# Three order edits around the last carry and the last merge of a hybrid RWKV-7 / neighbourhood-attention layer: one PSUM evacuation placed earlier, VectorE's order in the last gate written out by hand, one weight's low half made by an adding DMA

## The chip, the cores and the metric

The kernel runs on one core of a Trainium2 chip. The metric is the device time of one execution in microseconds, taken as the median of the runs shown. The engines have these names: PE is TensorE (matmul; PEld is its weight load), DVE is VectorE, ACT is ScalarE, POOL is GpSimd, SP is SyncE, which here does nothing but issue DMAs. Each engine works through its own queue in order.

## The reference, cut to what matters

One layer acts on 512 latent tokens and 128 context tokens, which the kernel treats as one block of 640 columns. The part that matters here is how the layer's two branches are merged:

```python
h = _rmsnorm(x, p["norm1_g"]) * (1.0 + sc1) + sh1
u_rw, u_na, gate_rw, gate_na = jnp.split(h @ p["w_in"], IN_SPLITS, axis=-1)
o_rw, s_new = _rwkv_branch(u_rw, s0, ...)
...
merged = (jax.nn.sigmoid(gate_rw) * (o_rw @ p["w_o_rwkv"])
          + jax.nn.sigmoid(gate_na) * (o_na @ p["w_o_na"]))
x = x + g1 * (merged @ p["w_out"])
h2 = _rmsnorm(x, p["norm2_g"]) * (1.0 + sc2) + sh2
x = x + g2 * ((jax.nn.silu(h2 @ p["ffn_w1"]) * (h2 @ p["ffn_w3"])) @ p["ffn_w2"])
```

The state recurrence inside `_rwkv_branch` runs forwards and backwards over the tokens, with a 64x64 state for each of 8 heads.

## The kernel before

All data is fp32. A product with a weight is made of three matmuls on operands split into a rounded high part and a low part (the rest): high times high, high times low and low times high. The weight's split is `wcast` (line 178). ACT writes the high half (`whi`, line 185). The low half (`wlo`) is made in one of two ways: by a DVE subtraction (line 188), or, where `eng is pool`, by ACT writing minus the weight's high part (line 183) and a DMA issued from POOL's queue that adds the weight itself (line 184). The weights come from HBM into `wst` buffers by DMAs on SP's queue (line 167), and a buffer is loaded anew once its readers are done.

The recurrence is done in chunks of 64 tokens for four pairs of heads, `ct` 0 to 3. For each pair there is a `carry` (line 1342): eight hops that pass the state from chunk to chunk. A hop is a short chain over engines: PE (L1367) into PSUM, ACT copies `x` (L1370), PE again (L1394), ACT copies `ZV` (L1400), PE (L1407, L1424), DVE multiplies the decay into the next `ZV` (L1419), and the next hop's PE work starts.

The hops leave PE idle, so the function `weave` (line 1560) puts other matmuls between their steps. They come from one long stream, `fill`, which makes projections, gates and the merges with `w_o`. The merge tasks are `merge_gen` (line 1509): matmuls into one of two PSUM buffers named `fl`, then an evacuation `rest` that frees the buffer, as `act.copy` into `mt` for the attention part (line 1524; the tiles of `mt` reuse others' memory and so carry names such as `kk` or `bv` in the profile) and as two DVE operations for the recurrence part (lines 1528 and 1530). An evacuation is not issued where its matmuls end. `later` puts it into the list `pend` with a delay counted in fill matmuls, and during a carry (`hold`) it is issued by `beside` at the places that the table `PRM["plan"]` sets: each step of the table is a number of fill matmuls, a dot, and a number that chooses a budget for ACT and DVE work (0 for none).

Behind the last carry (`ct` 3) comes its output stage (`out`, L1440 to L1455), then the last piece of the merge, here called the last gate, `last_gen` (line 1642). Sixteen times (8 tiles of 128 channels, two halves of 320 tokens), PE makes three matmuls into one of three PSUM buffers (L1652), DVE multiplies with the gate (L1653, which reads PSUM and so frees the buffer), DVE adds the sum so far (L1655, both inputs in SBUF), ACT rounds to the high part (L1656), and POOL subtracts to get the low part (L1657). The gates come back from HBM as `pre` and `tr` (L1646). From the sixth half on, two matmuls of the product with `w_out` (`acc`, L303, made by `tok_gen`) follow each half's three. The product is done in two passes of four weight pieces: `w_out[0]` to `w_out[3]` make output columns 0 to 511, `w_out[4]` to `w_out[7]` the rest. The first pass makes low halves by adding DMAs, the second by DVE.

What sets the order: inside a `manual_schedule` the named engines run in the order of the Python text, and every other engine's instructions are ordered by the tile framework's scheduler. For the last gate only PE is named (`MANUAL`).

Of the kernel before, what the change touches and what calls it, by code (L numbers as in the profile page):

```python
# [49 lines left out]
        ("0.0.0 16.1.0 8.1.1 9.0.0 2.1.0 8.1.1 13.1.1 0.1.1 0.1.1 0.1.1 0.1.0 6.1.0 6.1.0 6.1.0 6.1.0 "  # L50
         "6.1.0 6.1.0 7.1.0 6.0.0 6.0.0 6.0.0 6.0.0 6.0.0 6.0.0 7.0.0 6.0.0 6.0.0 6.0.0 6.0.0 6.0.0 "
         "6.0.0 6.0.0 11.0.0 8.0.0 8.0.0 2.0.0 0.0.0"),
        ("10.0 0.0 6.1 4.2 0.0 6.1 4.2 0.0 6.1 4.2 0.0 6.1 4.2 0.0 6.1 4.2 0.0 6.1 4.2 0.0 6.1 4.2 0.0 "
         "6.1 8.2 6.0"),
        "2 0 6 6 6 4 4 5 2 0 5 1 1 0 0"),
    qp=((0, 0, 7, 6, 7), (2, 5, 4, 4, 3, 2, 5, 3, 1)), ada=2, pa=1, pd=0,
# [21 lines left out]
MANUAL = {mybir.EngineType.PE}  # L78
# [29 lines left out]
def body(ctx: ExitStack, tc: tile.TileContext, xs, xp, cols, consts, w_ada, b_row, w_rw, w_qkv,  # L108
# [3 lines left out]
    pe, act, dve, pool, sp = nc.tensor, nc.scalar, nc.vector, nc.gpsimd, nc.sync  # L112
# [44 lines left out]
    def wdma(src, home=None):  # L157
        if len(rot) > 1 and home is None:
            rot.append(rot.pop(0))
        pl, nst, nhl = (rot if home is None else wpool)[-1 if home is None else home] if rot else wpool[-1]  # L160
        st = pl.tile([P, 1024], F32, tag="wst", bufs=nst, name=nm("wst"))
        n = src.shape[1]
        if len(src.shape) == 3:
            sp.dma_start(V(st[:, :], [[src.shape[2], n], [1, src.shape[2]]]), src)
            n *= src.shape[2]
        else:
            sp.dma_start(st[:, :n], src)
        return st, n, pl, nhl

    pend, off, hold, gtag = [], [0], [False], ["fl"]  # L170
# [7 lines left out]
    def wcast(w, eng=None):  # L178
        st, n, pl, nhl = w
        hi = pl.tile([P, 1024], F32R, tag="whi", bufs=nhl, name=nm("whi"))  # L180
        lo = pl.tile([P, 1024], F32R, tag="wlo", bufs=nhl, name=nm("wlo"))
        if eng is pool:
            act.activation(lo[:, :n], st[:, :n], AF.Copy, scale=-1.0)  # L183
            pool.dma_start(lo[:, :n].bitcast(F32), st[:, :n], accum_op=ALU.add)
        act.copy(hi[:, :n], st[:, :n])  # L185
        if eng is not pool:
            def low(a, b):
                dve.tensor_tensor(out=lo[:, a:b], in0=st[:, a:b], in1=hi[:, a:b].bitcast(F32), op=ALU.subtract)  # L188

            if len(gtag) > 1:  # L190
                low(0, 512)
                later(lambda: low(512, n), (0, 0), -off[0] + 5)
            else:
                low(0, n)
        return hi, lo

    def wload(src, eng=None):
        return wcast(wdma(src), eng)
# [22 lines left out]
    def drain(g):  # L221
        for _ in g:
            pass
# [50 lines left out]
    def tok_block(*args, **kw):  # L274
        pss = {}
        for _ in tok_gen(pss, *args, **kw):
            pass
        return pss
# [151 lines left out]
    def blkch(b):  # L430
        return [w_qkv[b * 4 + q] for q in range(4)]
# [74 lines left out]
    def tick(n):  # L506
        for p in pend:
            p[0] -= n
        while pend and pend[0][0] <= (-24 if hold[0] else 0):
            pend.pop(0)[2]()  # L510

    def beside(gen, budget):

        a = d = 0
        while a < budget[0] and d < budget[1]:
            if pend and pend[0][0] <= 0:
                _, c, fn = pend.pop(0)
                fn()
            else:
                c = next(gen, None)  # L520
                if c is None:
                    return
            a, d = a + c[0], d + c[1]
# [299 lines left out]
    with s1:  # L823
# [25 lines left out]
        with s1a:  # L849
            for b, dst, gcol in ((0, qT, dcol(dqg)), (1, kT, col("kg"))):  # L850
                pss = tok_block(pp, (hh, hl), blkch(b), list(range(8)), range(5)) if b else psq
# [44 lines left out]
            pss = tok_block(pp, (hh, hl), blkch(2), list(range(8)), range(5))  # L896
# [20 lines left out]
        with ExitStack() as s1b:  # L917
# [127 lines left out]
            with tc.manual_schedule(engines=FIRST):  # L1045
                for k, step in enumerate(PRM["na"].split()):
                    a, p, b, q, n = (int(x) for x in step.split("."))
# [29 lines left out]
    with ExitStack() as s3:  # L1077
# [482 lines left out]
        def weave(gen, others=(), bud=None):  # L1560

            for _ in (_ for g in ((0,), gen, (0,)) for _ in g):
                p = next(plan)
                for _ in range(p[0]):
                    if not next(fill, False):
                        break
                for o_, n in zip(others, p[1:]):
                    if bud:
                        if n:
                            beside(o_, bud[n - 1])  # L1570
                        continue
                    for _ in range(n):
                        next(o_, None)
                tick(PRM["tk"])
# [86 lines left out]
    def w_out_gen(pss, ws, toks, **kw):  # L1661
        return tok_gen(pss, pp, (mh, ml), ws, list(range(8)), toks, **kw)

    pss = {}
    trp = open_pool(hs, "trp")
    weights(hs, 2, 2)
    w0 = w_out_gen(pss, [c0] + [w_out[q] for q in range(1, 4)], range(5), eng=pool)
    with tc.manual_schedule(engines=MANUAL):
        for h, _ in enumerate(last_gen()):
            for _ in range(PRM["lw"][h]):  # L1670
                next(w0)
        drain(w0)
# [121 lines left out]

    with tc.manual_schedule(engines=FIRST):
        w1s = []
        beside(w_out_gen(pss, [w_out[4 + q] for q in range(4)], (0, 1, 2), tail=2, keep=w1s))
        beside(w_out_gen(pss, w1s, (3, 4), tail=2))
    hstack.close()

# [149 lines left out]
    with tc.manual_schedule(engines=FIRST):  # L1950
# [6 lines left out]
        for part, fs in enumerate(fts):  # L1957
# [13 lines left out]
            for n in range(2):  # L1971
                fin = part == len(fts) - 1 and n == 1
                pss = {}
# [121 lines left out]
```

## Time and profile before

| what | value |
|---|---|
| median of 3 runs | 1171.36 us (1169.81 to 1171.37) |
| the profiled execution, its own time | 1167.39 us |
| its span from first to last instruction | 1165.6 us |
| PE, PEld, DVE, ACT, POOL busy | 1119.1, 992.5, 778.7, 532.4, 191.2 us |
| mean granted TensorE clock | 0.995 |
| last carry (first hop's PE work to the last ACT copy of its output) | about 606.9 to 640.4 us |
| last gate (first to last of its matmuls) | 657.7 to 673.8 us |
| first matmul with `w_out` | 662.2 us |

The table's last three rows are read from the timeline. A row of the timeline gives the start and the length of one instruction or of a run of equal ones (x3), the engine, the line, the output and input tiles, and in brackets how long the engine had been idle before it and whose work ended that. The lengths of neighbouring matmuls overlap, so the distance between starts tells their pace. A row of the windows view gives a stretch, its length, and each engine's busy time with its count of instructions, then the granted PE clock, the busy share of the DMA engines and the bytes that they moved.

### The profile page before, as it was taken

The numbers are of one execution on the slowest core, as the hardware profiler recorded it, in microseconds if no ns is written. First come the engines' busy times: TensorE is split into PE (matmuls) and PEld (weight loads), VectorE is DVE, ScalarE is ACT, GpSimd is POOL, SyncE is SP. The second block draws the span as 40 slices with busy tenths as digits, with TensorE's granted clock in tenths as the row PEclk, the third lists the DMA queues.
The fourth block names the chain that finished last, engine by engine and source line by source line (L and its number), as shares of the span: only waits on it lengthen the run. The fifth ranks groups of instructions, "written<-read, shape, count | busy, mean of one in ns | idle before, by whom it ended". The sixth has DMA issues, their size and how long they took to land.

```text
span 1165.6 us, 26873 instructions
## 1 busy us (share of the span) xinstructions
PE 1119.1 (96%) x11160; PEld 992.5 (85%) x11160; DVE 778.7 (67%) x1642; ACT 532.4 (46%) x1051; POOL 191.2 (16%) x261
## 2 busy tenths in 40 slices
PE   6999999989999999999999899989999999999998
PEld 4688877788988988888898788989899989998997
DVE  4565365559558847946787856877568757875775
ACT  4444566555564565466442424644224423441330
POOL 1163244321101111120100331100000000001000
PEclk9999999999999999999999999999999999999999
DMA  9752777644423433343633772222212321232122
GB/s 337 262 117 82 226 250 227 200 134 115 123 64 94 136 94 91 87 125 85 249 111 114 233 218 75 88 73 91 90 57 89 107 87 61 75 107 91 55 84 97
DMA packets 60338, 148.63 MB, mean 128 GB/s; under 512 B 7444, under 2 KB 22420, under 8 KB 60216
## 3 DMA queue, kind: packets, MB, share of 16 engines
q1 hardware_dynamic: 55464, 131.56, 34.3%
q0 software_dynamic: 3888, 14.16, 6.3%
q8 instruction: 88, 1.44, 0.5%
q10 hardware_dynamic: 864, 1.20, 0.3%
q14 instruction: 34, 0.28, 0.1%
HBM read 118.41 MB, written 14.32 MB: 114 GB/s over the span
## 4 chain that ended last, share of the span: by engine, by line
PE 60%; DVE 8%; issue 6%; ACT 3%; DMA 1%; POOL 0%; SPq 0%; DVEq 0%; ACTq 0%; POOLq 0%
PE f L1814 22%; PE acc L303 17%; PE fl L216 10%; PE mm L216 1%; DVE pr L1293 1%; PE w L1394 1%; DVE RL L1297 1%; PE w L1367 1%; PE w L1191 1%; DMA o<-o_d 1%; PE w L1407 1%; PE w L1379 1%; PE w L1169 1%; ACT wlo L183 1%; DVE hq L1773 1%
## 5 line engine op out<-in xcount | busy, mean ns | idle before, releaser
L1814 PE MATMUL f<-t,whi 128*128 128x320 f32 x640 | 141.4, 309 | 0.0
L1814 PE MATMUL f<-b,whi 128*128 128x320 f32 x608 | 136.5, 312 | 3.6 <-ACT b L204 1.8
L303 PE MATMUL acc<-whi,u 128*128 128x512 f32 (+1 forms) x448 | 136.0, 385 | 0.0
L216 PE MATMUL fl<-h,whi 128*128 128x320 f32 x672 | 121.2, 320 | 1.0 <-issue 1.0
L1814 PEld LDWEIGHTS f<-t,whi 128*128 128x128 f32 x640 | 106.9, 188 | 0.0
L1814 PEld LDWEIGHTS f<-b,whi 128*128 128x128 f32 x608 | 102.9, 190 | 4.7 <-ACT b L204 2.2
L216 PEld LDWEIGHTS fl<-h,whi 128*128 128x128 f32 x672 | 101.3, 188 | 5.8 <-issue 1.2
L185 ACT CAST whi<-wst 128x1024 fp32r<-128x1024 f32 (+1 forms) x77 | 79.1, 1032 | 56.4 <-PE acc L303 42.4
L1814 PE MATMUL f<-t,wlo 128*128 128x320 f32 x320 | 98.9, 309 | 0.0
L303 PEld LDWEIGHTS acc<-whi,u 128*128 128x128 f32 x448 | 83.5, 188 | 16.6
L1814 PE MATMUL f<-b,wlo 128*128 128x320 f32 x304 | 94.8, 312 | 1.4 <-DVE wlo L1858 1.4
L1855 ACT CAST whi<-ws 128x1024 fp32r<-128x1024 f32 x40 | 42.0, 1050 | 108.9 <-PE f L1814 45.4
L303 PE MATMUL acc<-wlo,u 128*128 128x512 f32 (+1 forms) x224 | 86.3, 385 | 0.0
L188 DVE TENSOR_TENSOR wlo<-wst,whi 128x1024 fp32r<-128x1024 f32 (+2 forms) x58 | 62.0, 1080 | 35.0 <-ACT whi L185 34.5
L1869 POOL TENSOR_TENSOR ws<-wst 128x512 f32<-128x512 f32 x20 | 27.6, 1380 | 341.8 <-DVE wlo L1858 247.8
L303 PE MATMUL acc<-whi,h 128*128 128x512 f32 x240 | 78.0, 399 | 1.1 <-DVE h L428 1.1
L1691 DVE SCALAR_TENSOR_TENSOR tt<-acc,G 128x512 f32<-128x512 f32 (+1 forms) x51 | 34.7, 680 | 58.6 <-PE acc L303 58.6
L216 PE MATMUL fl<-h,wlo 128*128 128x320 f32 x336 | 63.4, 321 | 0.0
L1855 ACT CAST whi<-wst 128x1024 fp32r<-128x1024 f32 (+1 forms) x48 | 41.3, 869 | 42.3 <-PE acc L303 37.6
L1814 PEld LDWEIGHTS f<-t,wlo 128*128 128x128 f32 x320 | 60.1, 188 | 0.0
L1858 DVE TENSOR_TENSOR wlo<-ws,whi 128x1024 fp32r<-128x1024 f32 x40 | 54.7, 1367 | 6.6 <-ACT whi L1855 6.6
L1814 PEld LDWEIGHTS f<-b,wlo 128*128 128x128 f32 x304 | 57.6, 190 | 1.7 <-DVE wlo L1858 1.7
(342 smaller groups left out, 2499.9 us busy)
## 6 DMA issues: line engine op xcount, KB each, us to landing
wst<-in_w_dram SPq DMA_DIRECT2D x66, 512.0 KB
wst<-in_w_rw_dram SPq DMA_DIRECT2D x31, 512.0 KB
wlo<-wst POOLq DMA_DIRECT2D x27, 512.0 KB, 4.6
wa<-in_w_ada_dram SPq DMA_DIRECT2D x24, 512.0 KB
f<-in_w_ada_dram SPq DMA_DIRECT2D x16, 512.0 KB
wst<-in_w_qkv_dram SPq DMA_DIRECT2D x12, 512.0 KB
o<-o_d SPq DMA_DIRECT2D x14, 320.0 KB
x<-in_xs_dram SPq DMA_DIRECT2D x8, 512.0 KB
```

The costliest lines, as they stand in the source:

```text
L183: act.activation(lo[:, :n], st[:, :n], AF.Copy, scale=-1.0)
L185: act.copy(hi[:, :n], st[:, :n])
L188: dve.tensor_tensor(out=lo[:, a:b], in0=st[:, a:b], in1=hi[:, a:b].bitcast(F32), op=ALU.subtract)
L216: pe.matmul(ps[:, :t1 - t0], w[:, a:a + 128], x[:, k0 + kt, t0:t1], start=n == 0, stop=n == 3 * nk - 1)
L303: pe.matmul(pss[i][:, a:b], lhs(x, kt, ts_), w[:, cs_], start=ki == 0 and n == 0, stop=ki == last and n == 2)
L1169: pe.matmul(t[r0:r0 + 32, 64 * i:64 * i + 64], S.BK[l // 10][own, l % 10, 0, 32 * bk:32 * bk + 32], V(AG[own, l, h, :], [[0, 2], [1, 32]], ...
L1191: pe.matmul(pr[h][hrows[h ^ i], o_], x[hrows[h], :], R_[hrows[h], l, :], start=True, stop=True)
L1691: dve.scalar_tensor_tensor(out=tt, in0=ps[:, a:b], scalar=c, in1=G[:, g, sl], op0=ALU.mult, op1=ALU.mult)
L1814: pe.matmul(ps[:, :H2], w_[:, c_], x_[:, kt, :], start=first and kt + n == 0, stop=last and kt == 3 and n == 2, skip_group_check=more)
L1855: act.copy(r[0][:, :width], src())
L1858: dve.tensor_tensor(out=r[1][:, :width], in0=src(), in1=r[0][:, :width].bitcast(F32), op=ALU.subtract)
L1869: eng_x(PRM["se"][i - 1]).tensor_tensor(out=o_, in0=x, in1=y, op=op)
```

## The change

**The evacuation.** The table for the last carry begins with 10.3 where it had 10.0, and `weave` takes the new number 3 as: issue the first entry of `pend`, if it is due, at once.

**VectorE's order.** DVE joins PE in the manual schedule of `last_gen`.

**The weight.** `w_out[4]`, the first piece of the second pass, is loaded with `pool`, so its low half comes from an ACT instruction and an adding DMA in place of a DVE subtraction.

```diff
-        ("10.0 0.0 6.1 4.2 0.0 6.1 4.2 0.0 6.1 4.2 0.0 6.1 4.2 0.0 6.1 4.2 0.0 6.1 4.2 0.0 6.1 4.2 0.0 "
+        ("10.3 0.0 6.1 4.2 0.0 6.1 4.2 0.0 6.1 4.2 0.0 6.1 4.2 0.0 6.1 4.2 0.0 6.1 4.2 0.0 6.1 4.2 0.0 "
...
-                        if n:
+                        if n == 3 and pend and pend[0][0] <= 0:
+                            pend.pop(0)[2]()
+                        if 0 < n < 3:
                             beside(o_, bud[n - 1])
...
-    with tc.manual_schedule(engines=MANUAL):
+    with tc.manual_schedule(engines=MANUAL | {mybir.EngineType.DVE}):
...
-        beside(w_out_gen(pss, [w_out[4 + q] for q in range(4)], (0, 1, 2), tail=2, keep=w1s))
+        beside(w_out_gen(pss, [wload(w_out[4], pool)] + [w_out[4 + q] for q in range(1, 4)], (0, 1, 2), tail=2, keep=w1s))
```

PE's and SP's queues keep their order. Lines behind 1569 have numbers higher by two in the changed kernel. Three places show what moves. The first is ACT's queue at the first hop of the last carry (`kk` from `fl` is the evacuation; `x` and `ZV` are the hop's copies; `f` from `wos` is the split of a weight for the last gate). Before:

```order
L1338 COPY Rt<-w_8372 32x10x32
L1370 COPY x_1100_8448<-w_8439 128x256
L1400 COPY ZV<-w_8459 64x2x64 x4
L1524 COPY kk_8283<-fl_8352 128x320
L204 CAST f_1104_8480<-wos_8423 128x1024
L1524 COPY bv_8420<-fl_8421 128x320
```

After:

```order
L1338 COPY Rt<-w_8372 32x10x32
L1524 COPY kk_8283<-fl_8352 128x320
L1370 COPY x_1100_8449<-w_8440 128x256
L1400 COPY ZV<-w_8460 64x2x64 x4
L204 CAST f_1104_8480<-wos_8423 128x1024
L1524 COPY bv_8420<-fl_8421 128x320
```

The copy of `kk` moves ahead of the hop's five copies.

The second is DVE's queue at the head of the last gate. Before (`wlo` is the low half of `w_out[4]`):

```order
L1530 TENSOR_TENSOR bv_8420<-bv_8420,mx_9022 128x320
L188 TENSOR_TENSOR wlo_9473<-wst_9470,whi_9472 128x1024
L1653 SCALAR_TENSOR_TENSOR pre_9089<-pre_9089,fl_9105 128x320
L1653 SCALAR_TENSOR_TENSOR pre_9089<-pre_9089,fl_9113 128x320
L1653 SCALAR_TENSOR_TENSOR pre_9091<-pre_9091,fl_9121 128x320
L1655 TENSOR_TENSOR pre_9089<-mt_7728,pre_9089 128x320 x2
L1653 SCALAR_TENSOR_TENSOR pre_9091<-pre_9091,fl_9129 128x320
```

After:

```order
L1530 TENSOR_TENSOR bv_8420<-bv_8420,mx_9022 128x320
L1655 SCALAR_TENSOR_TENSOR pre_9089<-pre_9089,fl_9105 128x320
L1657 TENSOR_TENSOR pre_9089<-mt_7728,pre_9089 128x320
L1655 SCALAR_TENSOR_TENSOR pre_9089<-pre_9089,fl_9113 128x320
L1657 TENSOR_TENSOR pre_9089<-mt_7728,pre_9089 128x320
L1655 SCALAR_TENSOR_TENSOR pre_9091<-pre_9091,fl_9121 128x320
L1657 TENSOR_TENSOR pre_9091<-mt_7932,pre_9091 128x320
```

The subtraction is gone, and the sixteen multiplications and additions now strictly alternate to the end, where before up to three multiplications stood ahead of their additions.

The third is POOL's queue over the last gate. Before (`wlo_9063`, `wlo_9271` and `wlo_9308` belong to `w_out[0]`, `[1]` and `[2]`):

```order
L184 DMA wlo_9063<-wst_9060 128x1024
L1657 TENSOR_TENSOR m_9077<-pre_9089,m_9073 128x320 x2
L1657 TENSOR_TENSOR m_9077<-pre_9091,m_9073 128x320 x2
L1657 TENSOR_TENSOR m_9078<-pre_9093,m_9074 128x320 x2
L184 DMA wlo_9271<-wst_9268 128x1024
L1657 TENSOR_TENSOR m_9078<-pre_9095,m_9074 128x320
L184 DMA wlo_9308<-wst_9305 128x1024
```

After:

```order
L184 DMA wlo_9063<-wst_9060 128x1024
L184 DMA wlo_9470<-wst_9467 128x1024
L1659 TENSOR_TENSOR m_9077<-pre_9089,m_9073 128x320 x2
L1659 TENSOR_TENSOR m_9077<-pre_9091,m_9073 128x320 x2
L1659 TENSOR_TENSOR m_9078<-pre_9093,m_9074 128x320 x2
L1659 TENSOR_TENSOR m_9078<-pre_9095,m_9074 128x320
L184 DMA wlo_9271<-wst_9268 128x1024
```

The adding DMA of `w_out[4]` stands second, and the one of `w_out[1]` behind seven subtractions where it stood behind six. ACT's queue follows: the new instruction of `w_out[4]` (L183) stands between the two halves of `w_out[0]` and the high half of `w_out[4]`, ahead of all casts of the last gate, and the work for `w_out[1]` comes one cast later.

## The prediction

> **What bounds the kernel now.** I read the page's busy times first, then the windows view over the stretch that the change touches, then the timeline there.
>
> ```profile
> span 1165.6 us, 26873 instructions
> PE 1119.1 (96%) x11160; PEld 992.5 (85%) x11160; DVE 778.7 (67%) x1642; ACT 532.4 (46%) x1051; POOL 191.2 (16%) x261
> ```
>
> PE is busy 96% of the span, so an edit to the order of other engines can only win where PE waits, and what it can win in a stretch is PE's idle time there. The windows view (columns: stretch, length, PE, PEld, DVE, ACT, POOL busy with counts, PE clock, DMA share, GB/s):
>
> ```profile
> 601.00:612.00 11.00, 9.95 (x206) 8.88 (x198) 5.56 (x12) 5.74 (x15) 0.00 (x0) 1.00 0.28 86
> 657.70:664.30 6.60, 4.54 (x25) 3.39 (x23) 6.34 (x14) 2.16 (x4) 2.04 (x3) 1.00 0.78 228
> 664.30:674.10 9.80, 9.31 (x48) 7.62 (x49) 9.80 (x16) 6.86 (x12) 8.88 (x11) 1.00 0.69 181
> 674.10:693.00 18.90, 18.90 (x92) 15.49 (x91) 5.37 (x8) 4.30 (x7) 6.93 (x8) 1.00 0.83 250
> ```
>
> Around the first hop of the last carry PE idles 11.00 - 9.95 = 1.05 us. In the first part of the last gate it idles 2.06 us, in the rest of it 0.49 us, and from 674.1 on nothing. The clock is granted in full, so the idle time is waiting. All that the change can reach is about 3.6 us of 1171, or 0.3%; what follows asks how much of it comes free.
>
> **The evacuation before the hop.** The timeline of all engines there:
>
> ```profile
> 606.32 0.60 PE L216 MATMUL fl<-o,wlo 128*128 128x320 f32 x3
> ...
> 607.58 0.37 ACT L1370 COPY x<-w 128x256 f32<-128x256 f32 x1 [1.84 <-PE w L1367]
> ...
> 608.73 0.86 ACT L1400 COPY ZV<-w 64x128 f32<-64x128 f32 x4 [0.78 <-PE w L1394]
> 609.60 0.42 ACT L1524 COPY kk<-fl 128x320 f32<-128x320 f32 x1
> 609.92 1.05 ACT L204 CAST f<-wos 128x1024 fp32r<-128x1024 f32 x1
> ...
> 610.08 0.99 PE L216 MATMUL fl<-o,whi 128*128 128x320 f32 x5 [1.05 <-ACT kk L1524]
> ...
> 611.00 1.22 DVE L205 TENSOR_TENSOR f<-wos,f 128x1024 fp32r<-128x1024 f32 x1 [4.66 <-ACT f L204]
> ...
> 612.26 1.25 DVE L1419 TENSOR_TENSOR ZV<-w,Dt 64x128 f32<-64x128 f32 x4
> ```
>
> The matmuls whose result the `kk` copy takes end at 606.32 + 0.60 = 606.92, but the copy runs at 609.60, behind the hop's copies, and PE stands 1.05 us for its buffer. Moved ahead, the copy of 0.42 us runs from 606.92 to about 607.34, in time that ACT spent waiting: the `x` copy starts at 607.58 in any case. That leaves 0.24 us; if the copy started later than I take it, each tenth beyond that would go onto the hop's chain, at most 0.42 us.
>
> Of the 1.05 us not all stays won. The next thing late is the chain to the second hop: the cast of `f` on ACT, its low half on DVE, and only behind that, in DVE's order, the four multiplications into `ZV` (612.26, directly at the end of 611.00 + 1.22) for which PE's second hop waits. The copy was in front of that cast, so the chain gets earlier by its 0.42 us and no more. The lower bound is 0 (something between hides it again), the upper 1.05 us. I take **0.42 us**, since the row shows DVE with no gap before `ZV`. Behind it the fill matmuls fill PE to the end of the carry, so the gain should travel on (PE's 2.06 us of idle time in the gate wait for DVE, POOL and a DMA that ACT's work sets off).
>
> **VectorE's order in the last gate.** First DVE alone, then PE alone:
>
> ```profile
> 658.45 0.49 DVE L1530 TENSOR_TENSOR bv<-bv,mx 128x320 f32<-128x320 f32 x1
> 658.86 1.22 DVE L188 TENSOR_TENSOR wlo<-wst,whi 128x1024 fp32r<-128x1024 f32 x1
> 660.00 1.27 DVE L1653 SCALAR_TENSOR_TENSOR pre<-pre,fl 128x320 f32<-128x320 f32 x3
> 661.19 0.88 DVE L1655 TENSOR_TENSOR pre<-mt,pre 128x320 f32<-128x320 f32 x2
> 661.99 0.48 DVE L1653 SCALAR_TENSOR_TENSOR pre<-pre,fl 128x320 f32<-128x320 f32 x1
> 662.39 1.07 DVE L1655 TENSOR_TENSOR pre<-mt,pre 128x320 f32<-128x320 f32 x1
> ```
>
> ```profile
> 660.53 1.59 PE L1652 MATMUL fl<-o,f 128*128 128x320 f32 x9 [1.33 <-DVE pre L1653]
> ...
> 664.32 0.50 PE L303 MATMUL acc<-wlo,m 128*128 128x512 f32 x1 [0.21 <-DMA wlo<-wst]
> ...
> 664.88 0.60 PE L1652 MATMUL fl<-o,f 128*128 128x320 f32 x3
> ...
> 668.56 0.60 PE L1652 MATMUL fl<-o,f 128*128 128x320 f32 x3
> ...
> 670.01 0.71 PE L1652 MATMUL fl<-o,f 128*128 128x320 f32 x3 [0.39 <-DVE tr L1653]
> ...
> 673.17 0.60 PE L1652 MATMUL fl<-o,f 128*128 128x320 f32 x3
> ```
>
> With the subtraction of 1.22 us gone, the first multiplication starts at about 658.94 (658.45 + 0.49) instead of 660.00, and PE's wait of 1.33 us shrinks to a few tenths. But that does not make the product with `w_out` earlier: its third matmul reads the low half of `w_out[0]` and starts at 664.32, when the adding DMA has landed. Nothing in the change moves that landing except the 0.42 us from above. So PE only waits there longer, and what counts is the time behind it. There PE makes a half (three gate matmuls, two with `w_out`) every (668.56 - 664.88) / 4 = 0.92 us when it doesn't wait. The sixteenth half, eight behind the one at 664.88, would start at 664.88 + 8 x 0.92 = 672.2 without waiting and starts at 673.17. So the most to win is **1.0 us**.
>
> Is DVE fast enough for that? The groups of the gate on POOL and on DVE (count, busy us, mean ns):
>
> ```profile
> L1657 POOL TENSOR_TENSOR m<-pre,m 128x320 fp32r<-128x320 f32 x8 | 8.6, 1097 | 5.7 <-ACT m L1656 5.7
> L1655 DVE TENSOR_TENSOR tr<-P,tr 128x320 f32<-128x320 f32 x4 | 5.7, 1448 | 0.0
> L1655 DVE TENSOR_TENSOR pre<-mt,pre 128x320 f32<-128x320 f32 x8 | 5.2, 680 | 0.0
> ```
>
> An addition takes 0.48 us alone at best (0.88 for two) and 0.68 on average among the first eight, more when POOL subtracts at the same time; a multiplication goes on every 0.40 us. A pair costs 0.8 us undisturbed and 0.40 + 0.68 = 1.08 disturbed, against PE's 0.92. PE's sixteenth half needs the thirteenth multiplication (three buffers). Two pairs go undisturbed before POOL's first subtraction, so it ends at about 658.94 + 2 x 0.8 + 10 x 1.08 + 0.48 = 671.8, just ahead of 672.2. That would win the whole 1.0 us, but with 0.4 us to spare over twelve pairs; at 1.15 us for a pair only 0.6 is left, at 1.25 nothing. I take **0.6 us**, with bounds of a loss (below) and 1.0.
>
> **The weight's low half.** DVE's 1.22 us is counted above. New are an ACT instruction, a DMA issue on POOL and 512 KB of DMA:
>
> ```profile
> 657.29 0.60 PE L216 MATMUL fl<-o,wlo 128*128 128x320 f32 x3
> 657.49 1.05 ACT L185 CAST whi<-wst 128x1024 fp32r<-128x1024 f32 x1 [0.26 <-PE fl L216]
> ```
>
> ```profile
> 656.59 0.90 POOL L184 DMA_DIRECT2D wlo<-wst  x1 [8.99 <-DMA tr<-trw_d]
> 662.25 2.77 POOL L1657 TENSOR_TENSOR m<-pre,m 128x320 fp32r<-128x320 f32 x3 [4.77 <-ACT m L1656]
> ...
> 669.16 0.88 POOL L184 DMA_DIRECT2D wlo<-wst  x1
> ```
>
> ```profile
> 673.65 0.33 SPq L167 DMA_DIRECT2D wst<-in_w_out_dram  x1
> ```
>
> ACT's new instruction, taken at the 1.05 us of the cast, must wait for the last `wlo` matmuls of the merge (657.29 + 0.60 = 657.9), so both are done near 660.0; the gate's casts queue behind them, and the first of those can come at 659.9 at the earliest, so at most 0.1 us is lost, in front of a PE that is going to wait for the DMA anyway. POOL's 0.9 us falls into its idle 4.77 us. The DMA follows that of `w_out[0]` on the same queue, so it should not hold it up. SP's next load into the freed `wst` now waits for this landing rather than for DVE. The load behind it in SP's queue, `w_out[3]`, went out only at 673.65, which covers that. The `w_out[1]` DMA moves behind a seventh subtraction (about 1.1 us), and POOL starts about 1.8 us earlier; it was issued at 669.16, and of the first piece's 30 matmuls only 22 are done when the gate ends at 674.1, so it is read later than that. I take **0** for this edit. Without this cover it would cost up to 1.05 + 0.90 us; a gain beyond DVE's is excluded, as the first pass fills PE up to 693 (the windows view), and this weight belongs to the second.
>
> **Sum.** 0.42 + 0.6 + 0 = 1.0 us, on the profiled execution's own time 1167.39 - 1.0 = 1166.4 us. That execution lies 4.0 us below the median of the runs, 1171.36 us, so the forecast for the median is **1170.3 us**, 0.09% less.
>
> [...] How long the DMA of `w_out[0]` takes is in the issue view (microseconds to landing last), beside the one issued at 590.20, with the windows view of both:
>
> ```profile
> wlo<-wst POOLq DMA_DIRECT2D x1, 512.0 KB, 7.7
> ```
>
> ```profile
> wlo<-wst POOLq DMA_DIRECT2D x1, 512.0 KB, 4.4
> ```
>
> ```profile
> 590.20:594.30 4.10, 4.10 (x155) 3.91 (x157) 4.06 (x28) 1.82 (x4) 0.91 (x1) 1.00 0.67 132
> 656.60:659.70 3.10, 2.60 (x18) 2.34 (x17) 2.81 (x6) 1.68 (x2) 0.88 (x1) 1.00 1.01 392
> ```
>
> The slow one started with the DMA engines fully busy with loads (share 1.01, 392 GB/s), and DVE busy 2.81 of 3.10 us. The quick one had DVE busy 4.06 of 4.10 us and free DMA engines. So the loads, not DVE, go with the 3.3 us of delay, and the change leaves the loads as they are.
>
> [...]
>
> **The rivals.** *The landing moves* (15%). The subtraction at 658.86 lay in the stretch in which the DMA was late; if it is part of the 3.3 us, the DMA lands 1.2 us earlier or more, and PE goes on at once. That wins more only if DVE also keeps 0.8 us a pair, as otherwise the thirteenth multiplication bounds PE: 0.42 + 1.0 + 1.22 = 2.6 us, so 1168.7 us. For it: the overlap in time. Against it: the row at 590.20.
>
> *POOL holds DVE's additions* (22%). This one is slower than before. The row for it:
>
> ```profile
> 672.43 3.11 DVE L1655 TENSOR_TENSOR tr<-P,tr 128x320 f32<-128x320 f32 x1
> ```
>
> One addition took 3.11 us, while POOL subtracted three times in a row. Before, this fell behind the last multiplication that PE needed. In the strict alternation every multiplication stands behind an addition, so a held one stops PE as soon as the pair's time passes PE's 0.92 us and the three buffers are used up. One such hold costs 3.11 - 0.48 = 2.6 us; the thirteenth multiplication then ends at 671.8 + 2.6 = 674.4 and the sixteenth half starts 1.3 us later than 673.17; less 0.42 us that is 1172.2 us. Two make 1174.8 us. Midway stands 1173.5 us. Against it: with alternation POOL seldom has three subtractions ready at once.
>
> *Nothing arrives* (13%). The second hop, or a load late in the merge, takes back the first 0.42 us, and the pair's time eats the rest: 1171.4 us. The related case that the edit does nothing at all is excluded by the queues, in which the instructions do move.
>
> **How the numbers follow.** My forecast has the remaining 50%, with a range of its own from 1169.3 us (1.05 + 1.0 won) to 1171.4. About 0.2%, or 2.3 us, is what a measurement of this kernel can tell from no change. Faster by more than that are 14 of the 15 points of the first rival, and of the forecast 19, for the upper ends of both gains with the runs' own scatter of 1.6 us: 0.33. Slower by more are 13 of the 22 points of the second rival and 2 of the rest: 0.15. The other 0.52 are within. The range must leave out no more than 2 in 10: from 1167.6 us, a microsecond under the first rival, to 1173.0, short of two holds.
>
> **What would show it.** In the changed profile PE's wait for the `kk` copy is gone and a wait for `ZV` of up to 0.6 us stands before the second hop; from there all is 0.4 us earlier. The first multiplication of the gate follows the last addition of the merge with no gap; PE waits over 1 us for the low half of `w_out[0]` at its third matmul; the sixteenth half starts 8 x 0.92 us behind the half after that wait, or later by what the additions take over 1.1 us. The second rival shows as additions of 2 us or more ahead of the thirteenth multiplication. The forecast is wrong if that DMA lands in under 6 us, or if PE waits for DVE anywhere between 664 and 673.

## The result, and the profile after

| comparison | before, median | changed, median | ratio with its 95% interval |
|---|---|---|---|
| with the result (16 runs each) | 1168.71 us (1165.33 to 1171.70) | 1165.31 us (1162.21 to 1167.49) | 0.9975 (0.9963 to 0.9986) |
| f1_all (35 and 12 runs) | 1166.92 us | 1164.70 us | 0.9984 (0.9972 to 0.9996) |
| g4_all (35 and 12 runs) | 1167.40 us | 1165.67 us | 0.9978 (0.9964 to 0.9992) |
| h4_all (23 and 12 runs) | 1167.12 us | 1165.74 us | 0.9990 (0.9976 to 1.0004) |

The change is faster: three of the four intervals leave out 1. The mean of the four ratios is 0.9982, so about 2.1 us is won, against the 1.0 us forecast. The time of 1165.31 us also lies below the predicted range, which began at 1167.6 us: the 1171.36 us that the forecast started from was the median of three runs, and those three turned out to be the 12th, 14th and 15th of the 16 runs of before, sorted from the fastest to the slowest.

The page of the changed kernel (span, then busy time, share and count of each engine):

```profile
span 1160.4 us, 26874 instructions
PE 1118.1 (96%) x11160; PEld 991.4 (85%) x11160; DVE 776.7 (67%) x1641; ACT 533.7 (46%) x1052; POOL 193.7 (17%) x262
```

The three counts that moved are the edit's: DVE has one subtraction fewer, ACT and POOL have one instruction more. The windows view over the same four stretches as before (starting 3.2 to 4.5 us earlier; columns as before):

```profile
597.80:608.80 11.00, 10.65 (x210) 9.46 (x203) 5.85 (x13) 5.85 (x15) 0.00 (x0) 1.00 0.28 86
654.20:660.85 6.65, 4.73 (x25) 3.35 (x23) 6.22 (x14) 4.07 (x7) 4.74 (x5) 1.00 1.07 288
660.85:669.60 8.75, 8.71 (x48) 7.83 (x49) 8.47 (x16) 6.72 (x12) 8.55 (x10) 1.00 0.83 210
669.60:689.00 19.40, 19.40 (x94) 15.90 (x93) 4.82 (x7) 3.85 (x6) 6.45 (x7) 1.00 0.84 255
```

PE's idle time is length minus busy time: 0.35, 1.92, 0.04 and 0 us, where it was 1.05, 2.06, 0.49 and 0 us. The timeline shows what the hop and the gate wait for now:

```profile
602.46 0.41 ACT L1524 COPY kk<-fl 128x320 f32<-128x320 f32 x1
604.40 0.37 ACT L1370 COPY x<-w 128x256 f32<-128x256 f32 x1 [1.52 <-PE w L1367]
605.55 0.86 ACT L1400 COPY ZV<-w 64x128 f32<-64x128 f32 x4 [0.78 <-PE w L1394]
606.43 1.05 ACT L204 CAST f<-wos 128x1024 fp32r<-128x1024 f32 x1
...
607.51 1.23 DVE L205 TENSOR_TENSOR f<-wos,f 128x1024 fp32r<-128x1024 f32 x1 [4.35 <-ACT f L204]
...
608.76 1.25 DVE L1419 TENSOR_TENSOR ZV<-w,Dt 64x128 f32<-64x128 f32 x4
...
609.10 1.41 PE L1367 MATMUL w<-ZV,AG 128*64 128x64 f32 x16 [0.66 <-DVE ZV L1419]
```

```profile
654.25 1.48 PE L1654 MATMUL fl<-o,f 128*128 128x320 f32 x9
655.92 0.70 PE L1654 MATMUL fl<-o,f 128*128 128x320 f32 x3 [0.19 <-DVE pre L1655]
...
660.89 0.50 PE L303 MATMUL acc<-wlo,m 128*128 128x512 f32 x1 [1.32 <-DMA wlo<-wst]
...
661.46 0.60 PE L1654 MATMUL fl<-o,f 128*128 128x320 f32 x3
...
668.68 0.60 PE L1654 MATMUL fl<-o,f 128*128 128x320 f32 x3
```

The copy of `kk` is out of the hop, and PE's 1.05 us wait for it has become 0.66 us for `ZV`. In the gate PE waits 1.32 us for the low half of `w_out[0]`, and behind that it makes a half every (668.68 - 661.46) / 8 = 0.90 us without any wait.

To tell where the rest comes from, I cut each profile's span at four instructions. *Start* is the beginning of the last carry's first hop (all in front of it is the same in both kernels, but for the moved copy itself), *hop* runs from there to the gate's first matmul, *gate* from there to the first matmul of the sixteenth half, *behind* from there to the end. All times are starts in the timeline, in us:

| profile | edits | start | hop | gate | behind |
|---|---|---|---|---|---|
| before | none | 606.85 | 50.88 | 15.44 | 492.44 |
| e1_null | none | 608.47 | 50.88 | 15.45 | 492.41 |
| h1_null | none | 608.23 | 50.90 | 17.63 | 491.74 |
| h2_null | none | 607.46 | 50.88 | 15.41 | 492.40 |
| the changed kernel | all three | 603.66 | 50.59 | 14.43 | 491.75 |
| f1_all | all three | 609.22 | 50.57 | 14.21 | 492.42 |
| g4_all | all three | 604.74 | 50.58 | 14.21 | 492.51 |
| h4_all | all three | 612.28 | 50.57 | 14.27 | 492.49 |
| e2_evac | evacuation | 609.06 | 50.58 | 17.63 | 492.44 |
| e3_gate | order | 606.35 | 50.88 | 15.29 | 492.56 |
| e4_low | low half | 605.80 | 50.88 | 16.41 | 491.72 |
| f2_no_evac | order, low half | 605.53 | 50.88 | 14.57 | 491.72 |
| f3_no_gate | evacuation, low half | 604.26 | 50.57 | 14.29 | 492.01 |
| f4_no_low | evacuation, order | 605.84 | 50.58 | 15.30 | 491.78 |

Of the 5.2 us between the first two profiles compared (before and changed), 3.2 lie in front of the change, 0.3 in the hop, 1.0 in the gate, 0.7 behind it. The experiments ask which of these belong to the change.

### The profile page after: what moved, and what is told of

It reads as the page before. It is cut to its first block, busy times and chain, and to the rows that moved or that the text cites. A ratio compares the mean times of both kernels' runs of the same rounds, so it can differ in the third digit from the quotient of the medians.

```text
span 1160.4 us, 26874 instructions
## 1 busy us (share of the span) xinstructions
PE 1118.1 (96%) x11160; PEld 991.4 (85%) x11160; DVE 776.7 (67%) x1641; ACT 533.7 (46%) x1052; POOL 193.7 (17%) x262
## 4 chain that ended last, share of the span: by engine, by line
PE 58%; DVE 8%; issue 7%; ACT 3%; DMA 1%; POOL 0%; SPq 0%; DVEq 0%; ACTq 0%; POOLq 0%
PE f L1816 21%; PE acc L303 17%; PE fl L216 10%; DVE pr L1293 1%; PE mm L216 1%; DVE RL L1297 1%; PE w L1394 1%; PE w L1367 1%; DMA wlo<-wst 1%; PE w L1191 1%; DMA o<-o_d 1%; PE w L1407 1%; PE w L1379 1%; PE w L1169 1%; DVE AG L1148 1%
```

## The experiments

### One edit at a time

Three kernels take one of the three edits of the change and leave the other two. e1_null is the kernel before. e2_evac has

```diff
-                        if n:
+                        if n == 3 and pend and pend[0][0] <= 0:
...
```

with the two lines that follow it in the change and its table entry, e3_gate has

```diff
-    with tc.manual_schedule(engines=MANUAL):
+    with tc.manual_schedule(engines=MANUAL | {mybir.EngineType.DVE}):
```

and e4_low has

```diff
-        beside(w_out_gen(pss, [w_out[4 + q] for q in range(4)], (0, 1, 2), tail=2, keep=w1s))
+        beside(w_out_gen(pss, [wload(w_out[4], pool)] + [w_out[4 + q] for q in range(1, 4)], (0, 1, 2), tail=2, keep=w1s))
```

> The kernel before, unchanged. Two theories are tried in this group. Local: the change acts only through PE's waits between the last carry's first hop and the last gate's sixteenth half (call that stretch S; it is 673.17 - 606.85 = 66.32 us in the profile of before and 668.68 - 603.66 = 65.02 in that of the changed kernel), so some 1.3 us of the measured 2.9 are its doing, and the 3.2 us by which the changed profile is ahead at the start of S, in identical code, are scatter between executions. Upstream: that lead belongs to the changed program. Local expects here S = 66.3 +- 0.3, and the start of S anywhere between 603 and 608 us; ratio 1.000 +- 0.0015. Upstream expects the start of S near 606.9 again, as in before.

> Only the evacuation moved ahead of the hop. Local: PE's wait of 1.05 us for the kk copy is gone, one of 0.6 us for ZV stands before the second hop, S = 66.0 (0.3 to 0.4 less than before), ratio about 0.9997, not to be told from 1. Upstream: the start of S is below 605 if this edit is what moved it.

> Only VectorE's order fixed; the subtraction of 1.2 us stays in front of the gate on VectorE. Local: the multiplications start at the same place as before and each waits for an addition, so the thirteenth ends no earlier than before: S = 66.3, between 66.0 and 67.0, ratio 1.000. A rival within the local theory says that the alternation alone gives the gain of the gate: S = 65.3.

> Only the low half of w_out[4] by an adding DMA; VectorE's order in the gate is left to the scheduler, without the subtraction. Local: VectorE starts the gate about 1.1 us earlier, PE then waits over 1 us for the low half of w_out[0] and not for VectorE behind it: S = 65.4 to 65.9. The rival that the removed subtraction held up the adding DMA of w_out[0] expects that DMA to land in 6.5 us or less from its issue, where it took 7.7, and S near 65.

Measured against before (12 and 35 runs): 0.9993 (0.9979 to 1.0007), 0.9987 (0.9972 to 1.0001), 0.9986 (0.9973 to 1.0000) and 0.9989 (0.9973 to 1.0005). By the times none is told from no change.

The profiles say more. The hop is 0.30 us shorter wherever the evacuation is moved, and nowhere else. "Upstream" falls: in identical code the start lies anywhere from 603.7 to 612.3 us, with all edits (603.66, 609.22, 604.74, 612.28) as with none, a wider range than the 603 to 608 us that "local" gave. The order alone wins only 0.15 us in the gate. (This profile has 3.4 us at half the clock inside the gate, but f4_no_low below, at full clock, gives the same 15.3 us.) Two profiles missed every expectation: with the evacuation alone the gate took 17.63 us, and with the low half alone 16.41 us. The second has a simple reason, a stretch at half the clock inside the gate:

```profile
664.00:667.40 3.40, 3.40 (x11) 2.96 (x11) 1.34 (x4) 0.92 (x2) 2.20 (x3) 0.50 0.60 180
667.40:673.09 5.69, 5.69 (x33) 5.08 (x31) 5.66 (x12) 4.77 (x7) 4.46 (x6) 1.00 0.56 150
```

PE gets through 11 matmuls in 3.40 us there, against 33 in the 5.69 us behind it. The first, at a clock of 1.00, is taken up in the last group of experiments.

### One edit left out, and the part behind

f1_all is the changed kernel; f2_no_evac, f3_no_gate and f4_no_low each undo one of the three pieces shown above.

> The changed kernel again. Stretches: hop = first hop of the last carry to the gate's first matmul (50.88 us in the four profiles without the evacuation edit, 50.58 in the two with it); gate = first to sixteenth half (15.44 before, 14.43 changed); tail = sixteenth half to the end (492.4 where a half-speed window of the TensorE clock of 3.41 us falls on the matmuls behind the 1.77 us wait after the second pass, 491.7 where it doesn't). Theory A, three terms of which two are the change's: hop 50.6 and gate 14.4 in every execution, tail 491.7 or 492.4 by the phase of the clock's windows; ratio 0.9985 to 0.999. Theory B, the gate before is fragile: its old order gave 15.44, 15.45 and 17.63 us in three profiles of the same code, so on average it loses more than 1.0 us against a changed gate that stays at 14.4; ratio 0.9970 to 0.9980. Theory C, the adding DMA of w_out[4] itself wins the 0.7 us in the tail: tail 491.7 here and in every kernel with it.

> The changed kernel without the evacuation edit. All theories: hop 50.88. A and B: gate 14.4 (14.3 to 14.8). A: tail 491.7 or 492.4. C: tail 491.7. Ratio 0.0003 above that of the whole change.

> The changed kernel without VectorE's fixed order in the gate; the subtraction is gone, the scheduler sets VectorE's order. Hop 50.6. A: gate between 14.4 and 15.0, as VectorE starts 1.1 us earlier. B: gate anywhere from 14.4 to 17.6, by when POOL holds an addition ahead of a multiplication that PE needs. C: tail 491.7.

> The changed kernel with the low half of w_out[4] by VectorE's subtraction. Hop 50.6, gate 15.3 (as in the profile of the fixed order alone, 15.29). A: tail by chance 491.7 or 492.4. C: tail 492.4. Ratio about 0.0007 above that of the whole change by A and B, 0.0013 by C.

Measured (12 and 35 runs): 0.9984 (0.9972 to 0.9996), 0.9993 (0.9982 to 1.0004), 0.9994 (0.9981 to 1.0006), 0.9990 (0.9981 to 0.9999). The hop's 0.30 us goes with the evacuation again. The gate falls to 14.2 to 14.6 us in every kernel without the subtraction (but e4_low with its half-clock stretch) and stays at 15.3 us in both that keep it with the fixed order: the whole microsecond comes from the subtraction that is gone. f1_all against f4_no_low shows it best: with the same fixed order the gate is 14.21 us without the subtraction and 15.30 us with it. The ratio of f1_all, 0.9984, lies between what theories A and B gave and decides nothing between them.

In f3_no_gate and e4_low the scheduler sets DVE's order, but not the order of before: with the subtraction gone, it lets single multiplications and additions alternate from the seventh multiplication on. So these two don't test the old order without the subtraction.

The 0.7 us behind the gate is not the adding DMA's, so theory C falls: f1_all has that DMA and 492.42 us, f4_no_low has it not and 491.78 us. It is the place of a stretch at half the clock. Behind the second pass PE waits 1.77 us for the first split input of the next product (`b`); these are that wait and the clock behind it, in before and then in the changed kernel, and last a later stretch of the changed kernel:

```profile
729.85 0.41 PE L1814 MATMUL f<-b,whi 128*128 128x320 f32 x1 [1.77 <-ACT b L204]
```

```profile
730.80:734.20 3.40, 3.40 (x14) 3.40 (x14) 3.33 (x8) 1.18 (x3) 0.00 (x0) 0.50 0.30 113
```

```profile
725.38 0.41 PE L1816 MATMUL f<-b,whi 128*128 128x320 f32 x1 [1.77 <-ACT b L204]
```

```profile
726.50:729.90 3.40, 3.40 (x25) 3.40 (x24) 3.15 (x7) 1.36 (x3) 0.10 (x1) 1.00 0.36 113
```

```profile
759.30:762.70 3.40, 3.40 (x15) 3.40 (x14) 2.35 (x5) 1.61 (x4) 1.28 (x1) 0.50 0.47 154
```

The same wait is followed in one execution by 3.4 us at half the clock, with 14 matmuls in place of 25. In the other it is followed by full clock, and the 3.4 us at half the clock come 30 us later. Every profile here has one such stretch behind the gate, in ten of the eighteen at 728 to 735 us, in the others at 759 to 768 us. So the 0.7 us are the difference between the two places and not the price of a stretch: just behind the early one the part behind is 1.5 us longer in before than in the changed kernel (the same matmul starts 734.51 - 673.17 = 61.34 and 728.50 - 668.68 = 59.82 us after the sixteenth half), and the later one, in the changed kernel, takes part of that back. Ahead of the last 2 us of the span, the profile of before has three stretches at 0.50, from 246.12, 345.11 and 730.81 us, each 3.41 us long, and 1.00 between them; the starts lie 98.99 and 385.71 us apart, 29 and 113 times 3.413 us. That of the changed kernel has two, from 22.05 us for 6.83 us and from 759.33 us for 3.41 us, 737.28 us or 216 times 3.413 us apart.

### What limits the gate now

The thirteenth multiplication, whose buffer the sixteenth half needs, ends only 0.24 us before that half. DVE's timeline of the changed kernel, with the fourth, fifth and thirteenth multiplication, the fourth addition and a long one:

```profile
658.32 0.47 DVE L1655 SCALAR_TENSOR_TENSOR pre<-pre,fl 128x320 f32<-128x320 f32 x1
658.83 0.65 DVE L1657 TENSOR_TENSOR pre<-mt,pre 128x320 f32<-128x320 f32 x1
659.41 0.47 DVE L1655 SCALAR_TENSOR_TENSOR pre<-pre,fl 128x320 f32<-128x320 f32 x1
...
667.97 0.47 DVE L1655 SCALAR_TENSOR_TENSOR tr<-tr,fl 128x320 f32<-128x320 f32 x1
668.47 2.95 DVE L1657 TENSOR_TENSOR tr<-kk,tr 128x320 f32<-128x320 f32 x1
```

So two things seem to bound it at once: the DMA that PE waits for and DVE's pairs of 659.41 - 658.32 = 1.09 us. g1_hi takes the DMA's wait away, by issuing the products with the high half first (here `eng` is `pool` only in the first pass):

```diff
+            trips = [(ki, i, n) for ki, i in order for n in range(3)]
+            if eng is not None and ci == 0:
+                trips.sort(key=lambda t: (t[1] // 4, t[2] // 2))
...
```

g2_lag takes two additions from in front of the thirteenth multiplication; `rest` holds the addition, the cast and the subtraction of a half:

```diff
...
+                late.append(rest)
+                if len(late) > 2 * (c8 > 0):
+                    late.pop(0)()
```

g3_both has both, and g4_all is the changed kernel.

> The changed kernel with one edit more: in the first piece of the product with w_out the two products with the high half are issued for a group of tokens before the product with the low half, so that PE asks for the low half of w_out[0] at its seventeenth matmul and not at its third. In the changed profile PE waited 1.32 us there, and the thirteenth multiplication ended at 668.44, 0.24 us ahead of the sixteenth half that needs its buffer. Theory 'two limits at once': the DMA and DVE's pairs of 1.09 us bound the gate together, so taking the DMA's wait away moves it to DVE; the gate (first to sixteenth half, 14.43 us in the changed profile, 15.44 before) stays within 0.3 us of 14.4. Rival 'the DMA alone': the wait is what is left to win, the gate falls by 1.0 to 1.3 us to 13.1 to 13.4. In both the hop to the gate stays 50.6 us. Time against before: about -2.4 us by the first, -3.5 us by the second.

> The changed kernel with one edit more: in the last gate, from the third half on, DVE's addition (with its cast and subtraction) is issued two multiplications later. The thirteenth multiplication then stands behind ten additions and not twelve and ends 2 x 0.65 = 1.3 us earlier. Theory 'two limits at once': PE still waits for the DMA of w_out[0], now longer at its start of use, and runs at 0.905 us a half behind it; the gate stays within 0.3 us of 14.4. Rival 'DVE alone': the gate falls by 1.0 to 1.3 us. Rival 'POOL holds the additions': the lagged additions meet POOL's subtractions more often, one of 2 us or more falls ahead of the thirteenth multiplication, and the gate is 14.7 us or longer. Time against before: -2.4, -3.5 and -2 us or less.

> The changed kernel with both edits, the high half first and the additions two later. Theory 'two limits at once': only now is the gate shorter, by 1.0 to 1.3 us, 13.1 to 13.4 us, with PE at 0.905 us a half and no wait over 0.3 us; time against before about -3.5 us, against the changed kernel of this call about -1.2 us. Rivals 'the DMA alone' and 'DVE alone': no shorter than g1_hi or g2_lag. Rival 'POOL holds the additions': 14 us or longer, additions of 2 us or more ahead of the thirteenth multiplication.

> The changed kernel again, as the mark for the three others on the same chip. Hop to gate 50.6 us, gate 14.2 to 14.6 us, of which PE waits 1.3 us for the DMA of w_out[0]. The part behind the gate is 491.7 or 492.4 us, the latter if a half-speed window of TensorE's clock lies behind PE's wait at the end of the second pass. Time against before: 0.9975 and 0.9984 in the two comparisons so far, so -2 to -3 us.

| profile | gate | behind | ratio to before |
|---|---|---|---|
| g4_all | 14.21 | 492.51 | 0.9978 (0.9964 to 0.9992) |
| g1_hi | 14.21 | 492.51 | 0.9983 (0.9970 to 0.9995) |
| g2_lag | 13.96 | 493.50 | 0.9989 (0.9977 to 1.0002) |
| g3_both | 12.68 | 492.97 | 0.9979 (0.9967 to 0.9990) |

"Two limits at once" holds: each edit alone wins 0 and 0.25 us in the gate, both together 1.53 us, more than the 1.0 to 1.3 us expected (and g2_lag lies just below its 14.1 us). But the time missed its expectation, 0.9979 or about 2.5 us in place of 3.5 us, since the part behind grew with the late additions. (g4_all, g1_hi and g2_lag have their stretch at half the clock at 728 us, g3_both has it at 763 us.) In g3_both PE meets the next adding DMA, that of `w_out[1]`, which g4_all does not wait for:

```profile
670.67 0.60 PE L1658 MATMUL fl<-o,f 128*128 128x320 f32 x3
...
674.97 0.50 PE L306 MATMUL acc<-wlo,m 128*128 128x512 f32 x1 [0.95 <-DMA wlo<-wst]
```

g2_lag waits for the same DMA, 0.75 us.

### Is the gate of before steady, and is the next DMA the limit

h1_null and h2_null are the kernel before; h3_hi2 is g3_both with

```diff
-            if eng is not None and ci == 0:
+            if eng is not None and ci < 2:
```

and h4_all is the changed kernel.

> The kernel before, unchanged, for its profile. Two of its profiles had a gate of 15.44 and 15.45 us, three of the changed kernel 14.21 to 14.43 us; with the old order and the evacuation alone it was 17.63 us. Theory 'steady': the gate of before is 15.4 to 15.5 us whenever no half-speed clock window lies in it, and what the change wins is the 1.0 to 1.2 us of the gate and the 0.3 us of the hop, 1.3 to 1.5 us, the rest of the measured 2 to 3 us being scatter. Theory 'fragile': the gate of before is often 16.5 us or longer, because an addition of DVE is held ahead of the thirteenth multiplication, and the change wins 2 us or more on average.

> The kernel before once more, same question: 'steady' 15.4 to 15.5 us with the thirteenth multiplication unheld, 'fragile' 16.5 us or longer with a held addition ahead of it.

> g3_both with the high half first in the second piece, w_out[1], too. In g3_both the gate was 12.68 us against 14.21 us of the changed kernel in that call, but PE then waited 0.95 us for the adding DMA of w_out[1], where the changed kernel has no wait, and the part behind the gate, with no clock window in it, took 492.97 us against 491.75 us. Theory 'next DMA': that wait is what gave the gain back; now PE asks for the low half 3.6 us later, the wait is gone and the part behind is 491.7 to 492.0 us (492.4 to 492.7 with a clock window behind PE's wait at the end of the second pass), gate 12.5 to 12.9 us, time against the changed kernel of this call -1 to -1.5 us, against before about 0.997. Rival 'all the additions': the gain is lost to another wait (the subtractions on POOL end as late as in g3_both, and a product waits for the low half of m), the part behind stays at 492.6 us or more without a clock window.

> The changed kernel, as the mark for h3_hi2 on the same chip: gate 14.2 to 14.5 us, part behind it 491.7 us without and 492.5 us with a clock window behind PE's wait at the end of the second pass, time against before 0.9975 to 0.9984 as in three comparisons so far.

**The old gate has two forms.** h2_null gave 15.41 us and h1_null 17.63 us, the very figure of e2_evac, at full clock. So that was not the evacuation's doing: it is the same old order of DVE. The long form in PE's and DVE's timeline of h1_null:

```profile
672.76 0.72 PE L1652 MATMUL fl<-o,f 128*128 128x320 f32 x3 [1.63 <-DVE tr L1653]
...
675.75 0.71 PE L1652 MATMUL fl<-o,f 128*128 128x320 f32 x3 [0.90 <-DVE tr L1653]
```

```profile
669.42 0.47 DVE L1653 SCALAR_TENSOR_TENSOR tr<-tr,fl 128x320 f32<-128x320 f32 x1
...
670.51 1.80 DVE L1655 TENSOR_TENSOR tr<-P,tr 128x320 f32<-128x320 f32 x1
672.23 0.87 DVE L1653 SCALAR_TENSOR_TENSOR tr<-tr,fl 128x320 f32<-128x320 f32 x2
673.03 2.27 DVE L1655 TENSOR_TENSOR tr<-P,tr 128x320 f32<-128x320 f32 x2
675.22 0.87 DVE L1653 SCALAR_TENSOR_TENSOR tr<-tr,fl 128x320 f32<-128x320 f32 x2
```

and the same place in DVE's timeline of h2_null:

```profile
667.89 0.47 DVE L1653 SCALAR_TENSOR_TENSOR tr<-tr,fl 128x320 f32<-128x320 f32 x1
...
670.07 0.87 DVE L1653 SCALAR_TENSOR_TENSOR tr<-tr,fl 128x320 f32<-128x320 f32 x2
...
672.20 0.87 DVE L1653 SCALAR_TENSOR_TENSOR tr<-tr,fl 128x320 f32<-128x320 f32 x2
673.00 3.10 DVE L1655 TENSOR_TENSOR tr<-P,tr 128x320 f32<-128x320 f32 x1
```

The multiplications in these rows are the ninth, the tenth and eleventh, the twelfth and thirteenth. In h1_null long additions (1.80 us, and two in 2.27 us) stand between them, and PE waits 1.63 and 0.90 us. In h2_null the long one, 3.10 us, comes right behind the thirteenth and costs nothing.

A long addition goes with POOL's subtractions. These are POOL's rows of h1_null, of h2_null and of the changed kernel:

```profile
670.79 1.16 POOL L1657 TENSOR_TENSOR m<-pre,m 128x320 fp32r<-128x320 f32 x1
...
672.68 1.02 POOL L1657 TENSOR_TENSOR m<-pre,m 128x320 fp32r<-128x320 f32 x1
673.51 1.02 POOL L1657 TENSOR_TENSOR m<-tr,m 128x320 fp32r<-128x320 f32 x1
```

```profile
672.98 2.76 POOL L1657 TENSOR_TENSOR m<-tr,m 128x320 fp32r<-128x320 f32 x3
```

```profile
656.97 7.60 POOL L1659 TENSOR_TENSOR m<-pre,m 128x320 fp32r<-128x320 f32 x7 [0.29 <-ACT m L1658]
...
668.24 2.82 POOL L1659 TENSOR_TENSOR m<-tr,m 128x320 fp32r<-128x320 f32 x3
```

The long additions end 0.36 us behind POOL's subtraction or run of subtractions: 670.51 + 1.80 = 672.31 against 670.79 + 1.16 = 671.95 us, 673.00 + 3.10 = 676.10 against 672.98 + 2.76 = 675.74, 668.47 + 2.95 = 671.42 against 668.24 + 2.82 = 671.06. Subtractions that follow one another at once, as the two 0.83 us apart in h1_null, hold one addition until the last of them; the seven of the changed kernel, about 1.08 us apart, leave the additions at 0.65 us. That POOL does the holding is read from these times; no run took the subtractions off POOL.

What goes with the form is when the adding DMA of `w_out[0]` lands. These are the issue rows of h1_null, e2_evac, h2_null and e1_null:

```profile
wlo<-wst POOLq DMA_DIRECT2D x1, 512.0 KB, 6.8
```

```profile
wlo<-wst POOLq DMA_DIRECT2D x1, 512.0 KB, 6.9
```

```profile
wlo<-wst POOLq DMA_DIRECT2D x1, 512.0 KB, 8.2
```

```profile
wlo<-wst POOLq DMA_DIRECT2D x1, 512.0 KB, 7.8
```

The early landings, 6.8 and 6.9 us, go with the long gate, the late ones (7.7 us in before) with the short: after an early one PE goes on at once (h1_null and e2_evac have no wait for it, h2_null one of 0.76 us), and everything behind meets POOL at other moments. That is five executions, a link and not a proof. The four profiles of the changed kernel, with landings of 7.2 to 7.7 us, all have a gate of 14.21 to 14.43 us; none of them had a landing under 7 us, so they don't show that the changed kernel is safe from the long form.

**The next DMA.** In h3_hi2 the gate is 12.69 us and the 0.95 us wait is gone, but PE then waits for the next low half:

```profile
686.12 0.50 PE L306 MATMUL acc<-wlo,m 128*128 128x512 f32 x1 [0.37 <-DMA wlo<-wst]
```

The part behind is 492.20 us with the stretch at half the clock at the later place (759 us), 0.2 us over the expectation and under the rival's 492.6: of the 492.97 - 491.75 = 1.22 us that g3_both lost there, 0.77 came back, so most of the loss was the wait for the next DMA. The ratio to before is 0.9973 (0.9960 to 0.9986), the median 1164.08 us against 1165.74 us of h4_all (0.9990, outside the 0.9975 to 0.9984 expected, though its interval takes them in). It is faster than the kernel before; that it beats the changed kernel is likely by the profiles (gate 1.58 us shorter than in h4_all, part behind 0.45 us longer than the changed kernel's 491.75 us) but not settled by the times, whose intervals overlap.

## Why the prediction was wrong

Two terms were mis-sized: the base from which the 1.0 us was taken, and the gate. The mechanism of the gate was right for the form of the gate that the forecast had seen.

**The base.** The forecast took 1.0 us off 1171.36 us, the median of three runs, and counted with a scatter of 1.6 us, the spread of these three. Sixteen runs spread over 1171.70 - 1165.33 = 6.37 us, and over the five comparisons before has medians of 1166.9 to 1168.7 us. The forecast set its profiled run 4.0 us below that median and used the difference only as an offset, though it showed how far runs of this kernel lie apart. Of the miss, 1170.3 - 1165.31 = 4.99 us, the base makes 1171.36 - 1168.71 = 2.65 us, the larger part. The other 2.34 us are the 3.40 us between the medians of this comparison less the 1.0 us forecast. As the four comparisons give 2.1 us on average, about 1.3 us of that is the scatter of this one comparison, and 1.1 us is left for the terms of the sum.

**The hop, 0.42 us forecast, 0.30 us measured.** The mechanism was right: the `kk` wait is replaced by one for `ZV`, with the chain ACT's cast, DVE's low half, `ZV`. The size was the duration of the copy, 0.42 us, but the rows quoted show the next ACT instruction 609.92 - 609.60 = 0.32 us behind its start: the two overlap at their ends by 0.10 us, and the 0.30 us that the edit took out is nearer the distance between the starts. One reading was wrong without changing the sum: in the changed kernel the copy starts 603.66 - 602.46 = 1.20 us in front of the hop's first matmul, so the matmuls at 606.32, taken for its inputs, fill the other buffer.

**The gate, 0.6 us forecast, at most 1.0.** Point by point it went as written: the first multiplication follows the last addition of the merge at once, PE waits over 1 us (0.84 us in g4_all) at its third product, DVE's pairs take 1.09 us against the estimated 1.08 (by luck in part: the multiplication takes 658.83 - 658.32 = 0.51 and the addition 0.58 us, where 0.40 and 0.68 were put), the thirteenth multiplication ends just in time, the sixteenth half starts 8 x 0.90 us behind the wait. I took 0.6 for fear of pairs over 1.1 us; the full 1.0 to 1.2 us arrived. The edit that wins it is the weight's: with the subtraction kept, the fixed order gives 0.15 us. The step that failed is that the term, and its upper bound of 1.0 us, were read from a single profile of a gate with two forms. Over the four profiles of before the gate is (15.44 + 15.45 + 17.63 + 15.41) / 4 = 15.98 us, over the four of the changed kernel (14.43 + 14.21 + 14.21 + 14.27) / 4 = 14.28 us: 1.70 us. With the hop's 0.30 that is 2.0 us, as the mean ratio has it (2.1 us). Four profiles each, one long gate among them, give this share only roughly, so that the two figures agree so closely is partly chance.

**The low half, 0.** Right behind the gate: no cost is seen on ACT, POOL or SP, and the 0.7 us of the first profile behind it was the place of the half-clock stretch. With the subtraction's 1.22 us booked to the gate, the edits were told apart wrongly, not the sum.

**The rivals.** *POOL holds DVE's additions* is the mechanism that the times of the rows point to, but it costs time in the kernel before. In the changed profile the long addition (2.95 us at 668.47) comes behind the thirteenth multiplication; in h1_null two come ahead of it. The row of 3.11 us that I quoted for this rival was the harmless case of what the old order suffers from. *The landing moves*: in the four profiles of the changed kernel the DMA of `w_out[0]` took 7.7, 7.4, 7.2 and 7.6 us, in the four of before 7.7, 7.8, 6.8 and 8.2 us, 0.15 us less on average and not 1.2; and in the old order an early landing is the bad one. *Nothing arrives* fell with the hop's 0.30 us.

**Open.** Which of the two edits removes the long form, or whether they do: the two profiles with the fixed order and the subtraction had 15.3 us, the one without fixed order and subtraction at full clock 14.29 us, but in an order that isn't that of before, and all three at landings of 7.4 to 8.4 us. Why an early landing puts the long additions ahead was not tried.

## What to carry to other kernels

Where one execution's profile is the base, see first how far executions of the same code lie apart at an instruction in front of the change, and price the change by differences between instructions behind that point, in more than one profile of before. A waiting engine with a second limit 0.24 us away won little from either edit alone (0 and 0.25 us), and part of what both won together was held up again at the next transfer of the same kind. One and the same stretch of a kernel had two forms here (15.41 to 15.45 us in three profiles, 17.63 us in one), and what the change was worth there was the mean over both.

## What was not expected of the hardware

A stretch of identical code of about 605 us ended between 603.66 and 612.28 us. Part of this is the clock: the changed profile and h4_all, 8.6 us apart at that point, differ in the mean granted clock over the whole span, 0.995 and 0.989 (the lowest of all profiles, as in e1_null), and before was granted 0.95 from 230 to 262 us and 0.86 from 340 to 352 us, where the changed profile had 1.00; the other way round, the changed profile was granted 0.83 from 10 to 30 us, where before had 1.00. One half-clock stretch of 3.4 us, about 730 us in one execution and about 760 us in another, made 0.7 us between them. And a DMA that took 6.9 us to land in place of 7.8 us went with a gate that took 2.2 us longer.
